# A two-layer decoder trunk on one core: three orders of work shifted by steps (odd heads' scores, a head's first V tile, the roots of the latents' norms)

## The chip, the core and the metric

The kernel runs on one core of one Trainium2 chip. The metric is the device time of one execution in microseconds (us); each version is run several times and the median is compared. Beside the times there is one profiled execution, whose trace gives the start and length of every instruction on the engines: TensorE (PE, with its weight loads as PEld), VectorE (DVE), ScalarE (ACT), GpSimd (POOL) and SyncE (SP, which here only issues transfers).

## What is computed

Two layers over 512 tokens of width 2048, in float32. Layer 0 mixes tokens by retention with 8 heads, layer 1 by latent attention with 16 heads; each has a gate branch, and a condition vector shifts, scales and gates each layer. Cut to what bears on the change:

```python
# layer 0, per head (q, k: 512 x 256 after rotary turning; v: 512 x 512)
scores = (q @ k.T) * decay              # causal, decaying with distance
y = scores @ v
y = (y - mean(y)) * rsqrt(var(y) + EPS) # per token and head
out0 = (silu(g) * y * gn_g) @ w_out
# layer 1
cq, ckv, k_rope, g = split(h @ w_in)    # the latents: 512 x 512 each
q  = rmsnorm(cq, q_norm_g)  @ w_uq
kv = rmsnorm(ckv, kv_norm_g) @ w_ukv
```

## The kernel before

**Arithmetic.** Every float32 operand of a large product is split into a rounded high part and the rest, its low part (`split`, lines 134 to 136: a conversion on ScalarE, L135, then a subtraction on VectorE, L136). A product is three matmuls (`mm3`, lines 156 to 160): high by high (L158), high by low (L159), low by high (L160). The first factor is the loaded weight, the second the moving operand; in a head's values the scores are the weights and V moves, so L158 needs only the high part of a V tile and L159 its low part.

**Steps.** After the first projections the program is a list of `steps` (the class `Step`, line 749). A step has units of weights (a load and a `prepare`, which splits them), a `multiply` of mostly 24 matmuls of 512 columns, a `follow`, and lists of side work, `beside`, under the keys "load", "form" and "multiply". The loop at line 2180 writes each step in this order, and each part stands behind what its engines have already been given (`behind`):

1. SyncE: the weights up to three units ahead, then `beside["load"]`.
2. VectorE and ScalarE: `prepare_for(i + 1)`, the split of the next step's weights.
3. VectorE and ScalarE: `beside["form"]`.
4. TensorE: the step's own matmuls, then `beside["multiply"]`.
5. VectorE: sums of the modulation rows fetched a step before; then the `follow`.

Inside one such part the framework orders instructions by what it thinks is ready; across parts the order stands. Each engine works its queue in order, so VectorE and ScalarE may run ahead of TensorE until something that they need is missing.

**Retention beside the steps.** Heads 0 to 7 do their work beside other products, two heads to a block of 16 steps: the even head's 14 pieces (`retention`, line 1178; list at 1297) lie on steps 0 to 13 of the block, the odd head's on 4 to 17, so its last two reach into the next block (line 1620). Block 0 is the projection of the last q and k (lines 1324 to 1335); the next three are the output projection in rounds of four steps (`round_steps`, line 1412). At a round's end ScalarE copies each PSUM bank away and the next round's sums in (L1358, L1355). Where the pieces meet:

| step of the block | even head | odd head |
|---|---|---|
| 6 | load decay; scores | |
| 8 | load V; decay of the scores (L1223) | |
| 9 | load gates; split V; values | rotary turn |
| 10 | group norm: statistics, root on GpSimd, `yn` (L1262) | load decay; scores |
| 11 | gate (L1268) | |
| 12 | transposes `yT` (L1275) | load V; decay of the scores |
| 13 | output `o_h`, `o_l` (L1292, L1293) | load gates; split V; values |

Scores `s`, values `y` and transposes `yT` each take four PSUM banks out of one set of four (`aux`). Scores are 24 matmuls of 512 to 128 columns, values 30 of 512 columns.

**The latents.** Layer 1's latents, `q` and `kv`, are ready when the steps `g23` begin: eight steps for the third gate group (its products are `x_g`, `s_g`, `z_g`, `y_g`, its weights `g_00e` and so on) and eight for the fourth, 256 columns to a matmul. `latent_norm` (line 1770) stands in the form part of step 0 for `q` and of step 1 for `kv`: four squares with sums on ScalarE (L1775), and `rsqrt` (line 126), which is a small VectorE instruction (L129) and a power on GpSimd (L131). `latent_scale` (L1782, L1784) uses the result in steps 4 and 5.

Of the kernel before, what the change touches and what calls it, by code (L numbers as in the profile page):

```python
# [18 lines left out]
NT = T // P  # L19
# [30 lines left out]
def hybrid_trunk_kernel(  # L50
# [53 lines left out]
    def tmp(name, shape=(P, T)):  # L104
        return base.tile(list(shape), F32, tag="tmp", bufs=6, name=name)
# [7 lines left out]
    def small(name, n=1):  # L113
        return base.tile([P, n], F32, tag="small", bufs=24, name=name)
# [11 lines left out]
    def rsqrt(src, n, mul, name):  # L126

        v = small(f"{name}_v", n)
        DVE.tensor_scalar(out=v, in0=src, scalar1=mul, scalar2=EPS, op0=ALU.mult, op1=ALU.add)  # L129
        r = small(f"{name}_r", n)  # L130
        POOL.tensor_tensor(out=r, in0=v, in1=mhalf[:, :n], op=ALU.pow)  # L131
        return r

    def split(src, hi, lo):
        ACT.copy(hi, src)  # L135
        DVE.tensor_sub(lo, src, hi.bitcast(F32))  # L136
# [304 lines left out]
    A_, V_, T_, S_ = (getattr(mybir.EngineType, e) for e in ("Activation", "DVE", "PE", "SP"))  # L441

    @contextmanager
    def behind(*engines):

        with ExitStack() as stack:
            for e in engines:
                ins = next((i for i in reversed(nc.cur_bb.bb.instructions) if i.engine == e), None)
                if ins is not None:
                    stack.enter_context(tc.issue_after(ins))  # L450
            yield
# [76 lines left out]
    ss = [small(f"x_ss_{t}", 2) for t in range(NT)]  # L528
# [203 lines left out]
    def keep_rows(ps, dst_d, r0, name, func=AF.Identity, own=None):  # L732

        st = lpp.tile([P, T], F32, tag="st", bufs=2, name=name) if own is None else own(name)
        ACT.activation(st, ps, func)
        POOL.dma_start(dst_d[r0 : r0 + P, :], st)
# [12 lines left out]
    class Step:  # L749
# [3 lines left out]
        def __init__(self, load=None, prepare=None, multiply=None, follow=None, rows=0, sums=None):  # L753
            self.units = [(load, prepare)] if load else []
            self.multiply, self.follow = multiply, follow or (lambda: None)
            self.rows, self.sums = rows, sums
            self.beside = {"load": [], "form": [], "multiply": []}

    def plain_steps(nu, kn, parts, cn, name, take, n, lhs, rhs, evac, seeded=False, halved=0, **kw):

# [399 lines left out]
    def l1_tile(tag, bufs, name, shape=(P, T), dt=F32):  # L1160
        return pools["l1"].tile(list(shape), dt, tag=tag, bufs=bufs, name=name)
# [16 lines left out]
    def retention(h, own, own2=None):  # L1178
# [25 lines left out]
        def rope(n, j):  # L1204
            dst = (own2 or own)(f"qk_{h}_{n}_{j}p")
            rope_half(raws[f"qk{n}0"], raws[f"qk{n}1"], j == 1, dst, f"rope_{h}_{n}_{j}")
            qk.append(dst)
# [22 lines left out]
                    s_hl.append((spare[:, 0, 384:512], spare[:, 1, 384:512]))  # L1230
                split(st[:, :n], *s_hl[m])

        def split_v():
            for t in range(NT):
                v.append(own(f"v_{h}_{t}"))
                split(raws[f"v{t}"], v[t][:, 0, :], v[t][:, 1, :])

# [40 lines left out]
        def form_input():  # L1278
# [22 lines left out]
            {},  # L1301
            {"form": lambda: rope(1, 0)},
            {"form": lambda: rope(1, 1)},
            {"load": load_decay, "multiply": scores},
            {},
            {"load": load_v, "form": decay_scores},
            {"load": load_gates, "form": split_v, "multiply": values},
            {"form": group_norm},
            {"form": gate},
            {"multiply": transposes},  # L1310
# [14 lines left out]
    for h in (6, 7):  # L1325
# [3 lines left out]
            lambda b, ps, h=h: keep_rows(  # L1329
                ps, qk_d, (4 * h + b) * P, f"qk{h}_st{b}",  # L1330
                own=tmp,
            ),
# [154 lines left out]
    for u in range(4):  # L1487
        step = Step()
# [105 lines left out]
    for i, (multiply, follow) in enumerate(  # L1594
# [5 lines left out]
        step = Step(multiply=multiply, follow=follow)  # L1600
# [155 lines left out]
    latent = {}  # L1756
# [13 lines left out]
    def latent_norm(n):  # L1770
        if n == "q":
            DVE.tensor_scalar(out=qn_s, in0=qn_c, scalar1=192.0**-0.5, scalar2=None, op0=ALU.mult)
        ss = small(f"ss_{n}", NT)
        for t in range(NT):
            ACT.activation(tmp(f"{n}_sq{t}"), latent[n][t], AF.Square, accum_out=ss[:, t : t + 1])  # L1775
        latent[n, "r"] = rsqrt(ss, NT, 1.0 / 512, f"{n}_r")

    def latent_scale(n):
        for t in range(NT):
            r, v = latent[n, "r"][:, t : t + 1], latent[n][t]  # L1780
            if t % 2:
                ACT.activation(v, v, AF.Identity, scale=r)  # L1782
            else:
                DVE.tensor_scalar(out=v, in0=v, scalar1=r, scalar2=None, op0=ALU.mult)  # L1784
# [27 lines left out]
    def g2_seven(gi):  # L1812


        def load_half(u, odd_, j):
            c0 = 1088 + gi * T + j * H
            return w_mla_in[:, c0 : c0 + H].rearrange("(u i e p) n -> u e p i n", i=2, e=2, p=P)[u, odd_]

        def finish(x, s, y, m4, m5):
            def store(j, half, t):  # L1820
                r0 = (gi * 4 + 2 * j) * P
                POOL.dma_start(
                    sg2_d[r0 : r0 + 2 * P, half * H : (half + 1) * H].rearrange("(b p) n -> p b n", p=P),
                    t.rearrange("p (b n) -> p b n", b=2),
                )

            for j, ps in enumerate((x, s)):
                st = tmp(f"sgs_{gi}_{j}")
                ACT.activation(st, ps, AF.Silu)
                store(j, 0, st)  # L1830
            for j, m in enumerate((m4, m5)):
                DVE.tensor_add(m, m, y)
                ACT.activation(m, m, AF.Silu)
                store(j, 1, m)

        return seven_rows_steps(
            f"g2{gi}", load_half, h2, sums2, *turns2, finish, lambda second, u: 0,
            ((False, 0),) if gi == 2 else ((False, 3), (True, 1)),
        )

    g23 = g2_seven(2) + g2_seven(3)

    for n, g_c, at in (("q", qn_s, (0, 4, 10, 11)), ("kv", kvn_c, (1, 5, 12, 13))):
        g23[at[0]].beside["form"].append(lambda n=n: latent_norm(n))
        g23[at[1]].beside["form"].append(lambda n=n: latent_scale(n))
        g23[at[2]].beside["multiply"].append(lambda n=n: latent_transposes(n))
        g23[at[3]].beside["form"].append(lambda n=n, g_c=g_c: latent_parts(n, g_c))
# [316 lines left out]
    def prepare_for(i):  # L2164
        units = steps[i].units if i < len(steps) else ()
        with behind(V_, A_):
            for _, prepare in units:
                prepare()
        return len(units)
# [10 lines left out]
    for i, step in enumerate(steps):  # L2180
        if i == n_p:
            lp.__exit__(None, None, None)
            l1 = tc.tile_pool(name="l1", bufs=1)
            pools["l1"] = l1.__enter__()
            l1_tile("gap", 1, "gap", (P, EVEN))
        if i == n_l2:
            l1.__exit__(None, None, None)
            l2 = tc.tile_pool(name="l2", bufs=1)
            pools["l2"] = l2.__enter__()
            l2_ready.append(pair_tile(pools["l2"], "own", "own_pair2"))  # L2190
        with behind(S_):
            while n_loaded < min(n_prepared + 3, len(loads)):
                loads[n_loaded]()
                n_loaded += 1
            if i in (n_p, n_l2):
                pool, tables, n0 = (pools["l1"], rotary, 0) if i == n_p else (pools["l2"], rotary2, 2)
                for n, name in enumerate(("cos", "sin")):
                    tables.append(rot(pool, f"{name}_{n0}"))
                    nc.sync.dma_start(tables[n], tables_d[(n0 + n) * P : (n0 + n + 1) * P, :])
            for load in step.beside["load"]:  # L2200
                load()
        n_prepared += prepare_for(i + 1)
        with behind(V_, A_):
            for form_ in step.beside["form"]:
                form_()
        with behind(T_):
            step.multiply()
        with behind(T_):
            for multiply in step.beside["multiply"]:
                multiply()  # L2210
        with behind(V_, A_):
            ahead = 2 if i < n_p - 2 else 1
            for j, add in list(fetched):
                if j + ahead <= i:
                    add()
                    fetched.remove((j, add))
            if step.sums is not None:
                form_sums(step.sums, hT, sums1, staged1, more1)
        if i + 1 < len(steps):
            for _ in range(steps[i + 1].rows):  # L2220
                with behind(S_):
                    fetched += [(i, f) for f in (next(later, None),) if f is not None]
        with behind(V_, A_, T_):
            step.follow()
# [274 lines left out]
```

## Time and profile before

| | |
|---|---|
| median of three runs | 2140.48 us (2140.27 to 2141.76) |
| the profiled execution | 2141.7 us |
| its span, first to last instruction | 2139.9 us |
| mean granted clock of TensorE | 0.998 |

The page of the profile gives busy times and their share of the span. A line of a timeline reads: start in us, length in us, engine, line of the kernel, operation, what is written <- what is read (buffer numbers left out), the shape, how many were merged, and in brackets the engine's idle time ahead and what ended it. A line of the waits reads: who waited <- for whom: us in total, times, longest. Matmuls overlap: one of 512 columns is shown 0.39 us long, but the next one starts well before it ends. So the time that a wait costs is read from start to start.

### The profile page before, as it was taken

To read this page: it belongs to the slowest core of one execution; us is meant where nothing else is said; L and a number is where in the kernel's file an instruction comes from. 1 tells how busy PE (TensorE), PEld (TensorE's weight loads), DVE (VectorE), ACT (ScalarE), POOL (GpSimd) and SP (SyncE) were. 2 spreads that over 40 slices of the span, in tenths; PEclk is the share of its full clock that TensorE was granted. 3 is DMA by queue.
4 is the path that set the end of the run, shared out by engine and by line. 5 is a ranking of instruction groups with operands and counts; after the bars stand their busy time and mean duration, and the time that the engine had idled before them with its cause. 6 is when DMAs were issued, how large, how long until landed. Compare 5 with 4: busy or idle time off the path is not lost. (4 is left out here: it accounts for less than half of the span.)

```text
span 2139.9 us, 29960 instructions
## 1 busy us (share of the span) xinstructions
PE 2114.4 (99%) x11100; PEld 1814.4 (85%) x11100; DVE 1676.8 (78%) x2481; ACT 1054.2 (49%) x1604; POOL 106.4 (5%) x178
## 2 busy tenths in 40 slices
PE   8999999999999999999999999999999999999998
PEld 5887898988888888888888888898889989988887
DVE  7898788888979789666777777668978788886745
ACT  5764444444444544434344544445446565664434
POOL 1000000000000000000000000010001000000000
PEclk9999999999999999999999999999999999999999
DMA  9975687878788778855647566553466644346734
GB/s 382 398 279 193 219 290 229 278 242 262 256 262 265 240 235 277 264 174 192 236 152 249 182 210 240 168 177 113 163 189 205 188 127 148 119 133 221 246 104 143
DMA packets 229781, 462.95 MB, mean 216 GB/s; under 512 B 20817, under 2 KB 84337, under 8 KB 225793
## 3 DMA queue, kind: packets, MB, share of 16 engines
q1 hardware_dynamic: 217424, 421.85, 60.2%
q0 software_dynamic: 11920, 38.91, 4.7%
q8 instruction: 87, 1.43, 0.3%
q14 instruction: 60, 0.49, 0.1%
q10 hardware_dynamic: 290, 0.27, 0.0%
HBM read 417.96 MB, written 43.00 MB: 215 GB/s over the span
## 5 line engine op out<-in xcount | busy, mean ns | idle before, releaser
L1407 PE MATMUL o<-o_h,o_p 128*128 128x512 f32 (+1 forms) x1088 | 323.4, 378 | 0.0
L1407 PEld LDWEIGHTS o<-o_h,o_p 128*128 128x128 f32 x1088 | 199.8, 188 | 37.9 <-DVE o_p L136 1.0
L1407 PE MATMUL o<-o_l,o_p 128*128 128x512 f32 (+1 forms) x544 | 204.8, 376 | 0.0
L1407 PEld LDWEIGHTS o<-o_l,o_p 128*128 128x128 f32 x544 | 102.3, 188 | 18.4
L136 DVE TENSOR_TENSOR o_p<-o_r,o_p 128x1024 fp32r<-128x1024 f32 x64 | 78.1, 1223 | 48.5 <-ACT o_p L135 48.2
L2335 PE MATMUL o<-o_h,o_w 128*128 128x512 f32 (+1 forms) x320 | 82.2, 346 | 0.0
L135 ACT CAST o_p<-o_r 128x1024 fp32r<-128x1024 f32 x64 | 66.5, 1051 | 26.4 <-PE o L1407 15.0
L160 PE MATMUL qk<-hT,qk_p 128*128 128x512 f32 x192 | 75.4, 393 | 1.5 <-DVE qk_p L136 1.5
L158 PE MATMUL qk<-hT,qk_p 128*128 128x512 f32 x192 | 75.8, 395 | 0.0
L159 PE MATMUL qk<-hT,qk_p 128*128 128x512 f32 x192 | 75.3, 392 | 0.0
L378 DVE SCALAR_TENSOR_TENSOR aw<-aw,c_all 128x2048 f32<-128x2048 f32 (+1 forms) x35 | 73.1, 2102 | 2.8 <-DMA aw<-in_ada_t_dram 2.6
L1109 DVE SCALAR_TENSOR_TENSOR mod<-mod,c_odd 128x1024 f32<-128x1024 f32 x48 | 58.0, 1220 | 20.1 <-DMA mod<-in_ada_t_dram 20.1
L2335 PEld LDWEIGHTS o<-o_h,o_w 128*128 128x128 f32 x320 | 55.9, 189 | 7.5
L1109 DVE SCALAR_TENSOR_TENSOR mod<-mod,c_bm 128x1024 f32<-128x1024 f32 x48 | 58.5, 1218 | 0.0
L135 ACT CAST o_h<-o_in 128x1024 fp32r<-128x1024 f32 x24 | 25.2, 1050 | 64.5 <-PE o L159 46.7
L136 DVE TENSOR_TENSOR o_l<-o_in,o_h 128x1024 fp32r<-128x1024 f32 x24 | 29.3, 1222 | 34.1 <-ACT o_h L135 34.1
L2335 PE MATMUL o<-o_l,o_w 128*128 128x512 f32 (+1 forms) x160 | 55.3, 346 | 0.0
L136 DVE TENSOR_TENSOR o_w<-o_w_raw,o_w 128x1024 fp32r<-128x1024 f32 x32 | 38.9, 1220 | 19.0 <-ACT o_w L135 19.0
L1262 ACT ACTIVATE yn<-y,nmr,gn_r 128x512 f32<-128x512 f32 x32 | 22.3, 777 | 62.7 <-DVE nmr L1256 62.7
L159 PE MATMUL o<-o_l,o_w 128*128 128x512 f32 x128 | 50.0, 391 | 0.3 <-DVE o_l L136 0.3
L158 PE MATMUL o<-o_h,o_w 128*128 128x512 f32 x128 | 50.1, 392 | 0.0
L160 PE MATMUL o<-o_h,o_w 128*128 128x512 f32 x128 | 49.9, 390 | 0.0
(1534 smaller groups left out, 6333.6 us busy)
## 6 DMA issues: line engine op xcount, KB each, us to landing
mod<-in_ada_t_dram SPq DMA_DIRECT2D x96, 512.0 KB, 6.0
o_r<-in_ret_w_out_dram SPq DMA_DIRECT2D x64, 512.0 KB, 5.5
aw<-in_ada_t_dram SPq DMA_DIRECT2D x30, 1024.0 KB, 8.9
mod_gate<-in_ada_t_dram SPq DMA_DIRECT2D x32, 512.0 KB, 5.0
o_w_raw<-in_mla_w_out_dram SPq DMA_DIRECT2D x32, 512.0 KB, 4.3
qk_r<-in_ret_w_in_dram SPq DMA_DIRECT2D x48, 256.0 KB, 3.1
qk_r<-qk_d SPq DMA_DIRECT2D x32, 256.0 KB, 6.2
v_r<-v_d SPq DMA_DIRECT2D x32, 256.0 KB, 6.3
```

The lines of the kernel that those rows point to most:

```text
L135: ACT.copy(hi, src)
L136: DVE.tensor_sub(lo, src, hi.bitcast(F32))
L158: PE.matmul(o, lhs[0], rhs[0], start=first and not seeded, stop=False, skip_group_check=seeded)
L159: PE.matmul(o, lhs[0], rhs[1], start=False, stop=False, skip_group_check=seeded)
L160: return PE.matmul(o, lhs[1], rhs[0], start=False, stop=last, skip_group_check=seeded)
L378: DVE.scalar_tensor_tensor(out=aw[:, cols], in0=aw[:, cols], scalar=1.0, in1=c_all[:, cols], op0=ALU.mult, op1=ALU.mult, accum_out=col[:, ...
L1109: DVE.scalar_tensor_tensor(out=aw, in0=aw, scalar=1.0, in1=silu_c[j], op0=ALU.mult, op1=ALU.mult, accum_out=mc[:, j, b : b + 1],)
L1262: ACT.activation(y, ys[i], AF.Identity, bias=nmr[:, i : i + 1], scale=r[:, i : i + 1])
L1407: PE.matmul(o, w[i][:, ki, c0 + b * P : c0 + (b + 1) * P], a[j], start=first and i + j == 0, stop=last and i == 1, skip_group_check=True,)
L2335: PE.matmul(banks2[b][:, cols], w[0][i][:, 0, b * P : (b + 1) * P], o2_moving(w, u, cols)[j], start=u + i + j == 0, stop=u == KD - 1 and i ...
```

## The change

Three shifts; no arithmetic is added or taken away.

1. Of the retention's pieces, `scores` of the odd heads moves from the odd head's piece 6 to piece 7, that is from the end of step 10 of a block to the end of step 11. `load_decay` stays. The even heads stay as they were.
2. `split_v` takes the tiles to be split. A new list `beside["early"]` is written ahead of `prepare_for(i + 1)`. The first V tile of each head is split there, the other three where all four were.
3. `latent_norm` ends at the squares. Its `rsqrt` becomes `latent_root`, in the form part two steps later (step 2 for `q`, step 3 for `kv`).

```diff
-            self.beside = {"load": [], "form": [], "multiply": []}
+            self.beside = {"load": [], "early": [], "form": [], "multiply": []}
...
-        def split_v():
-            for t in range(NT):
+        def split_v(ts):
+            for t in ts:
...
-            {"load": load_decay, "multiply": scores},
-            {},
+            {"load": load_decay} if h % 2 else {"load": load_decay, "multiply": scores},
+            {"multiply": scores} if h % 2 else {},
             {"load": load_v, "form": decay_scores},
-            {"load": load_gates, "form": split_v, "multiply": values},
+            {"load": load_gates, "early": lambda: split_v((0,)), "form": lambda: split_v((1, 2, 3)), "multiply": values},
...
-        latent[n, "r"] = rsqrt(ss, NT, 1.0 / 512, f"{n}_r")
+        latent[n, "ss"] = ss
+
+    def latent_root(n):
+        latent[n, "r"] = rsqrt(latent[n, "ss"], NT, 1.0 / 512, f"{n}_r")
...
         g23[at[0]].beside["form"].append(lambda n=n: latent_norm(n))
+        g23[at[0] + 2].beside["form"].append(lambda n=n: latent_root(n))
...
+        with behind(V_, A_):
+            for form_ in step.beside["early"]:
+                form_()
         n_prepared += prepare_for(i + 1)
```

## The prediction

> **What bounds the kernel now.** I read the page first, then the waits of TensorE and of its weight loads, then the timelines of TensorE, ScalarE and VectorE where a wait was named.
>
> ```profile
> span 2139.9 us, 29960 instructions
> PE 2114.4 (99%) x11100; PEld 1814.4 (85%) x11100; DVE 1676.8 (78%) x2481; ACT 1054.2 (49%) x1604; POOL 106.4 (5%) x178
> PE s L158 <- ACT yn L1262: 1.5, 4, 0.5
> PEld y L159 <- DVE v L136: 1.3, 3, 0.6
> PEld x_g L924 <- DVE g_03e L960: 0.3, 1, 0.3
> ```
>
> TensorE is the bound; only time in which it waits can be won. The edits concern three waits: the scores of the four odd heads (s), which wait for the normalisation of the even head before them; the values (y), which wait for a V tile's low part; and one product of the third gate group (x_g), which waits for weights. Idle time understates such a wait, because matmuls overlap. I measure from start to start:
>
> ```profile
> 966.45 0.39 PE L159 MATMUL qk<-hT,qk_p 128*128 128x512 f32 x1
> 966.67 0.39 PE L160 MATMUL qk<-hT,qk_p 128*128 128x512 f32 x1
> 967.53 0.50 PE L158 MATMUL s<-qk_0p,qk_0p 128*128 128x512 f32 x1 [0.47 <-ACT yn L1262]
> 967.87 0.39 PE L159 MATMUL s<-qk_0p,qk_0p 128*128 128x512 f32 x1
> ...
> 1192.48 0.39 PE L1407 MATMUL o<-o_h,o_p 128*128 128x512 f32 x1
> 1193.22 0.50 PE L158 MATMUL s<-qk_0p,qk_0p 128*128 128x512 f32 x1 [0.36 <-ACT yn L1262]
> 1193.56 0.40 PE L159 MATMUL s<-qk_0p,qk_0p 128*128 128x512 f32 x1
> ```
>
> Undisturbed matmuls of 512 columns start 0.23 us apart (966.45 to 966.67; more finely 0.227, which I use). Head 1's scores start 0.86 us after their predecessor, 0.63 too late, and the next start is 0.34 on, 0.11 too late: 0.74. Head 5: 0.51 + 0.11 = 0.62. The idle of all four is 1.5, less head 1's 0.47 leaves 0.34 each for the rest, so heads 3 and 7 are as head 5. **Scores: 0.74 + 3 x 0.62 = 2.60 us.**
>
> ```profile
> 1179.59 0.39 PE L1407 MATMUL o<-o_h,o_p 128*128 128x512 f32 x1
> 1179.90 1.19 PE L158 MATMUL y<-v,sT 128*128 128x512 f32 x4
> 1181.24 0.50 PE L159 MATMUL y<-v,sT 128*128 128x512 f32 x1 [0.15 <-DVE v L136]
> ...
> 1293.31 0.39 PE L1407 MATMUL o<-o_h,o_p 128*128 128x512 f32 x1
> 1294.96 0.50 PE L159 MATMUL y<-v,sT 128*128 128x512 f32 x1
> ```
>
> Heads 4 and 6 wait for their first V tile. From 1179.59 to 1181.24 lie five steps, 1.14 us; it took 1.65, so 0.51 is lost, and 0.11 behind it as above. Head 6 (1293.31 to 1294.96) is the same. **Values: 2 x 0.62 = 1.24 us.**
>
> ```profile
> 1628.16 0.84 PE L924 MATMUL y_g<-sums,g_02o 128*128 128x256 f32 x6
> 1628.84 1.35 PE L924 MATMUL x_g<-h,g_03e 128*128 128x256 f32 x7
> ```
>
> Six matmuls take 0.84 us, so five steps and a 0.28 matmul, 0.11 a step; seven would be 0.95 and took 1.35. **Third gate group: 0.40 us.** All three together: 4.24 us, which is the most that the edits can win directly.
>
> **Scores of odd heads.** Nothing is added: 24 matmuls go behind the next step's 24. No DMA moves. They waited for PSUM banks that the even head's normalisation still read:
>
> ```profile
> 1192.39 2.78 ACT L1262 ACTIVATE yn<-y,nmr,gn_r 128x512 f32<-128x512 f32 x4 [5.87 <-DVE nmr L1256]
> 1198.73 0.59 ACT L1358 COPY x<-o 128x512 f32<-128x512 f32 x1 [2.62 <-PE o L1407]
> 1203.96 1.04 ACT L135 CAST o_p<-o_r 128x1024 fp32r<-128x1024 f32 x1
> 1206.17 0.68 DVE L1223 TENSOR_TENSOR s_0f<-s,dec 128x512 f32<-128x512 f32 x1
> 1208.97 0.28 DVE L1223 TENSOR_TENSOR s_3f<-s,dec 128x128 f32<-128x128 f32 x1
> 1208.06 1.91 PE L1275 MATMUL yT<-ident,yn 128*128 128x128 f32 x16
> ```
>
> The normalisation ends at 1195.2. The next step would start at 1192.48 + 0.23 = 1192.7 and last 24 x 0.227 = 5.45, so the scores would start at 1198.2: banks free 3 us earlier. The full 2.60 goes. Next late could be the even head's transposes (yT) one step on, which take over the banks of the scores. Scores run 3.7 us (1193.22 to the next step near 1197.1, less the 0.1 restart), so to 1201.9; a step and three of four transposed banks later (5.45 + 1.3) the fourth bank is due at 1208.6. VectorE's decay took from 1206.17 to 1209.25, 3.1 us. It stood behind the 1203.96 conversion, and that behind the round's bank copies, which wait for TensorE (1198.73) and so move up by 3.7 + 0.7 = 4.4 us; behind the normalisation and one conversion they then begin near 1196.1 and, eight of 0.6, end at 1201. Conversion and subtraction (1.05 + 1.2) give 1203.2, the decay ends at 1206.3: 2.3 us of cover. Queued behind the decay on VectorE are a modulation sum, the V split, the next weights and the even head's output; the next consumer is the values at 1201.9 + 5.45 + 1.7 + 5.45 = 1214.5, and that row of work has shorter cover only if the decay stays on its old clock (a rival).
>
> **First V tile ahead of the next weights.** One conversion and one subtraction per head change places with the weights' pair; no instruction and no transfer is added.
>
> ```profile
> 1178.28 1.05 ACT L135 CAST o_p<-o_r 128x1024 fp32r<-128x1024 f32 x1
> 1179.23 2.17 ACT L135 CAST v<-v_r 128x512 fp32r<-128x512 f32 x4
> ...
> 1180.50 2.49 DVE L136 TENSOR_TENSOR v<-v_r,v 128x512 fp32r<-128x512 f32 x4
> ...
> 989.82 0.39 PE L159 MATMUL y<-v,sT 128*128 128x512 f32 x1
> ```
>
> In head 4 tile 0 would be converted at 1178.3 to 1178.9 and subtracted by 1179.7; the values want its low part at 1179.8 + 0.23. That wait goes. But tile 1 is no earlier: its conversion, the weights' pair and tile 0 all still stand ahead of it. Its low part ended at 1180.50 + 2 x 0.60 + 0.09 = 1181.79. Today four products of tile 0 are put first, which hides it; with tile 0 early the order may become the plain one (six products with tile 0, then tile 1), and the eighth is due at 1179.8 + 7 x 0.227 = 1181.4. So 0.37 + 0.11 of wait comes back per head, or 0 if the order stays. I take the returning wait, because head 1, where V is early, already runs in the plain order (its second product, at 989.82, is one with a low part, L159): 1.24 - 2 x 0.48 = **0.3 us**, ends 0.3 and 1.24. The weights behind it come 0.6 to 0.7 us later; they are wanted after 30 value products, 6.8 us.
>
> [...]
>
> **Roots two steps later.** VectorE stood at them:
>
> ```profile
> 1620.06 0.17 DVE L129 TENSOR_SCALAR q_r_v<-ss_q 128x4 f32<-128x4 f32 x1 [1.16 <-ACT q_sq L1775]
> 1625.92 0.17 DVE L129 TENSOR_SCALAR kv_r_v<-ss_kv 128x4 f32<-128x4 f32 x1 [1.24 <-ACT kv_sq L1775]
> 1628.06 1.22 DVE L960 TENSOR_TENSOR g_03e<-g_03e_r,g_03e 128x1024 fp32r<-128x1024 f32 x1
> 1620.31 1.41 POOL L131 TENSOR_TENSOR q_r_r<-q_r_v,few 128x4 f32<-128x4 f32 x1 [82.48 <-DVE q_r_v L129]
> 1636.19 1.33 ACT L1782 ACTIVATE q<-q,q_r_r 128x512 f32<-128x512 f32 x2
> ```
>
> The subtraction ending at 1629.28 is what x_g waits for. Without both idles it can be up to 2.4 us earlier, and 0.4 is enough. The root itself (0.17 on VectorE, 1.41 on GpSimd, no other work of GpSimd between) would end near 1630 against its use at 1636.19. **0.40 us.**
>
> **Sum:** 2.60 + 0.3 + 0.40 = 3.3 us. On the profiled execution (2141.7 us, of which 1.8 lie around its span) that gives 2138.4; it stands 1.2 above the median of the three runs, so the forecast is 2140.48 - 3.3 = **2137.2 us**. About 0.2%, 4.3 us here, is what a measurement of this kernel tells from no change; the forecast is below that.
>
> **Rivals.** (1) *Everything goes*: tile 1 is not late, 4.24 us, 2136.2, a hair from the bound. For: heads 0 and 2 run the same order without a wait. Against: tile 1 has no earlier place. (2) *The transposes take over the wait*: if the decay keeps its old clock, its end at 1209.25 just met the fourth bank (1208.06 + 1.3 = 1209.3); TensorE then arrives 0.6 earlier and waits that long in heads 3, 5 and 7: 3.3 - 1.8 = 1.5 won, 2139.0. Against: the bank copies follow TensorE. (3) *Slower: the early V tile holds the weights.* Place: the conversion queue ahead of the step behind the values, all eight heads.
>
> ```profile
> 1166.52 2.49 SPq L1185 DMA_DIRECT2D v_r<-v_d  x4
> 1201.81 2.22 SPq L1185 DMA_DIRECT2D v_r<-v_d  x4
> DMA to landing us min/median/max: 4.1/6.3/7.4
> ...
> 163.50 0.50 PE L160 MATMUL qk<-hT,qk_p 128*128 128x512 f32 x1 [1.54 <-DVE qk_p L136]
> ...
> 165.46 0.63 PE L160 MATMUL qk<-hT,qk_p 128*128 128x512 f32 x1
> 165.88 0.63 PE L158 MATMUL qk<-hT,qk_p 128*128 128x512 f32 x1
> ```
>
> It decides once V lands later than the next step less 2.3 us of splitting: for head 4 at 1187.1 - 2.3 = 1184.8 (26 products behind 1181.24; V issued at 1166.52, so 18 us), for head 5 at 1214.5 + 6.8 - 2.3 = 1219 (17 us), against 7.4 at most. If it did so by 1.5 us each, a wait as at 163.50 (1.54) would cost 1.7, and behind that one eight matmuls ran 0.42 apart instead of 0.23, 1.6 more: 8 x 3.3 - 3.0 = 23 lost, 2164. [...] The row shows the slow spacing after 1.5 us; I go by the row. (4) *The edits don't reach their waits* (something else ends last at the same places): 2140.5.
>
> **Chances.** Forecast 0.52, (1) 0.22, (2) 0.14, (3) 0.05, (4) 0.07. Rival 1 lies on the bound and half of it counts as faster, with 0.04 for small waits that vanish beside: faster 0.15; slower 0.05 and 0.01 for accidents of a new instruction order: 0.06; within 0.2%: 0.79. The range: below, rival 1 less the half microsecond by which runs differ, 2135.6; above, rival 2 and as much again, 2139.8.
>
> **What would show it.** Right: no wait of s on yn; step 11 of each block follows step 10 at 0.23; scores directly behind; yT without idle; y of heads 4 and 6 with at most 0.4 of a wait, on tile 1's low part; VectorE without the idles of 1.16 and 1.24 ahead of the roots; x_g at 0.11 spacing. Wrong: a wait of yT on the decay, of y on sT, of o on its weights after the values, or scale waiting on the root.

## The result, and the profile after

The changed kernel takes 2135.76 us in the median of 13 runs, beside 2141.14 us for 13 runs of the kernel before: a ratio of 0.9975, 95% interval 0.9968 to 0.9982. That is 5.4 us faster. The forecast was 3.3 us and its range ends at 2135.6, so the time stands at the range's fast edge. The likeliest of the three outcomes, a time within 0.2%, was missed by a hair (0.25% faster, and the interval spans the bound).

The profiled execution took 2134.56 us. The head of its page, and, in the second fence, a line of its waits:

```profile
span 2132.8 us, 29957 instructions
...
PE 2109.9 (99%) x11100; PEld 1814.8 (85%) x11100; DVE 1677.6 (79%) x2481; ACT 1052.8 (49%) x1604; POOL 106.0 (5%) x178
```

```profile
PEld o L159 <- DVE o_l L136: 1.8, 2, 1.0
```

Of the three waits shown of before, s on yn and x_g on g_03e are gone from this list. A wait of 0.3 us of y on v is left of 1.3, in the weight loads alone: no matmul of y idles. The line above has grown from 0.7 us in before to 1.8: the last output waits for the low parts of its inputs (o_l), in a part that no edit touches. TensorE's busy time fell by 4.5 us (from 2114.4) for the same 11100 matmuls: most of the gain never stood as idle.

**The scores of head 5** (timeline of TensorE, after):

```profile
1194.17 0.39 PE L1407 MATMUL o<-o_l,o_p 128*128 128x512 f32 x1
1194.40 0.39 PE L1407 MATMUL o<-o_h,o_p 128*128 128x512 f32 x1
1194.62 0.39 PE L158 MATMUL s<-qk_0p,qk_0p 128*128 128x512 f32 x1
1194.85 0.39 PE L159 MATMUL s<-qk_0p,qk_0p 128*128 128x512 f32 x1
...
1203.65 0.39 PE L1407 MATMUL o<-o_h,o_p 128*128 128x512 f32 x1
1203.88 1.91 PE L1275 MATMUL yT<-ident,yn 128*128 128x128 f32 x16
```

Step 11 stands between, and the scores follow it at 0.22 and 0.23 us; before, the first came 0.74 behind its predecessor (1192.48 to 1193.22). The transposes also follow at 0.23. What they take over is the bank of the last decay (timeline of VectorE, after):

```profile
1202.94 0.28 DVE L1223 TENSOR_TENSOR s_3f<-s,dec 128x128 f32<-128x128 f32 x1
```

It ends at 1203.2, and the fourth bank is due at 1203.88 + 1.3 = 1205.2: 2.0 us of cover.

**The values of head 4, and the last rows of head 7** (timelines of VectorE and of TensorE, after):

```profile
1176.10 0.68 DVE L136 TENSOR_TENSOR v<-v_r,v 128x512 fp32r<-128x512 f32 x1
1176.97 1.23 DVE L136 TENSOR_TENSOR o_p<-o_r,o_p 128x1024 fp32r<-128x1024 f32 x1 [0.18 <-ACT o_p L135]
1178.11 1.89 DVE L136 TENSOR_TENSOR v<-v_r,v 128x512 fp32r<-128x512 f32 x3
...
1323.37 1.88 DVE L136 TENSOR_TENSOR v<-v_r,v 128x512 fp32r<-128x512 f32 x3
```

```profile
1176.91 0.39 PE L158 MATMUL y<-v,sT 128*128 128x512 f32 x1
...
1178.04 0.39 PE L160 MATMUL y<-v,sT 128*128 128x512 f32 x1
1178.27 0.62 PE L158 MATMUL y<-v,sT 128*128 128x512 f32 x2
1178.72 0.62 PE L159 MATMUL y<-v,sT 128*128 128x512 f32 x2
1179.19 0.63 PE L160 MATMUL y<-v,sT 128*128 128x512 f32 x2
...
1322.98 0.39 PE L158 MATMUL y<-v,sT 128*128 128x512 f32 x1
```

Tile 1's low part is ready at 1178.11 + 0.69 = 1178.80. After six products in plain order come pairs: two of L158, two of L159. The first L159 starts at 1178.72, too early for tile 1, so it is tile 0's; tile 1's is the tenth product, at 1178.95, and just in time. Head 7 runs in plain order: there tile 1 is ready at 1323.37 + 0.69 = 1324.06, and its low part is due as the eighth product, at 1322.98 + 7 x 0.227 = 1324.57, 0.5 us later.

**The third gate group** (timeline of VectorE, after, then of TensorE after, then of TensorE before):

```profile
1619.44 1.23 DVE L960 TENSOR_TENSOR g_03e<-g_03e_r,g_03e 128x1024 fp32r<-128x1024 f32 x1
...
1621.71 0.16 DVE L129 TENSOR_SCALAR q_r_v<-ss_q 128x4 f32<-128x4 f32 x1
```

```profile
1622.75 1.52 PE L924 MATMUL x_g<-h,g_03e 128*128 128x256 f32 x12
1624.11 1.52 PE L924 MATMUL y_g<-sums,g_03o 128*128 128x256 f32 x12
...
1640.43 1.52 PE L924 MATMUL x_g<-h,g_13o 128*128 128x256 f32 x12
1641.79 1.52 PE L924 MATMUL s_g<-sums,g_13o 128*128 128x256 f32 x12
```

```profile
1632.03 1.58 PE L924 MATMUL s_g<-sums,g_03e 128*128 128x256 f32 x12
1633.44 1.57 PE L924 MATMUL z_g<-h,g_03o 128*128 128x256 f32 x12
...
1640.51 1.58 PE L924 MATMUL y_g<-sums,g_11e 128*128 128x256 f32 x12
1641.92 1.57 PE L924 MATMUL s_g<-sums,g_11o 128*128 128x256 f32 x12
```

VectorE does not stand at the root, and g_03e ends 2.1 us ahead of its use. But look at the distance between one line of twelve and the next. After: 1.36 us, or 113 ns a matmul. Before, behind the wait of x_g: 1.41 us, or 118 ns, and that still ten microseconds on. Start by start, 332 matmuls ran at 118 there, from 1629.6 to 1668.5, until the latents' transposes come; after, none did. 332 x 4.7 ns = 1.5 us, beside the 0.38 of the wait itself.

**Where the 7.1 us between the two profiles came from.** For this and the experiments I add up, over a stretch (in us from the span's start), by how much each matmul starts later than the columns of the one before it ask for (0.227 us for 512, 0.113 for 256). The texts ahead of the experiments call this the excess. The last two columns are stretches that the change does not touch.

| kernel | time to before, 95% interval | 900–1400 (retention) | 1590–1700 (gate groups) | 150–185 | 2000–2060 |
|---|---|---|---|---|---|
| before | | 5.23 | 2.25 | 3.73 | 0.60 |
| after | 0.9975 (0.9968–0.9982) | 0.59 | 0.40 | 2.10 | 1.56 |
| after, second profile | 0.9975 (0.9965–0.9985) | 1.52 | 0.39 | 2.11 | 0.63 |
| scores alone | 0.9991 (0.9982–1.0) | 2.62 | 2.29 | 2.10 | 0.91 |
| early V alone | 0.9998 (0.9989–1.0007) | 4.79 | 2.25 | 2.09 | 0.61 |
| roots alone | 0.9991 (0.9982–1.0) | 5.01 | 0.39 | 2.11 | 1.27 |
| after + 5 additions | 0.9979 (0.997–0.9988) | 1.04 | 2.79 | 2.09 | 1.58 |
| after + 4 additions | 0.9984 (0.9975–0.9992) | 2.05 | 2.30 | 2.10 | 2.48 |
| + 5 and transposes | 0.9983 (0.9974–0.9992) | 2.55 | 1.67 | 3.71 | 1.49 |
| root of q back | 0.9968 (0.9956–0.9981) | 0.70 | 0.39 | 3.70 | 3.79 |
| gate sums behind | 0.9966 (0.9954–0.9978) | 2.16 | 0.40 | 2.11 | 0.01 |
| early V in even heads | 0.9969 (0.9957–0.998) | 0.69 | 0.42 | 2.12 | 1.59 |
| the last two | 0.9963 (0.9949–0.9976) | 0.59 | 0.40 | 3.70 | 1.80 |
| odd V a step earlier | 1.007 (1.0057–1.0082) | 21.10 | 0.37 | 2.10 | 1.11 |

Retention gave 4.6, the gate groups 1.9, the stretch at 150 to 185 gave 1.6 by luck (below), and the last output took 1.0 back: 7.1.

### The profile page after: what moved, and what is told of

Its sections match the earlier page's. It is cut to its first block, busy times and chain, and to the rows that moved or that the text cites. A ratio compares the mean times of both kernels' runs of the same rounds, so it can differ in the third digit from the quotient of the medians.

```text
span 2132.8 us, 29957 instructions
## 1 busy us (share of the span) xinstructions
PE 2109.9 (99%) x11100; PEld 1814.8 (85%) x11100; DVE 1677.6 (79%) x2481; ACT 1052.8 (49%) x1604; POOL 106.0 (5%) x178
## 4 chain that ended last, share of the span: by engine, by line
PE 90%; DVE 4%; DMA 3%; issue 2%; ACT 1%; POOL 0%; SPq 0%; DVEq 0%; POOLq 0%; ACTq 0%
PE o L1407 16%; PE o L2342 4%; PE s L825 2%; PE y L826 2%; PE y L825 2%; PE y L827 2%; PE s L826 2%; PE s L827 2%; PE x L826 2%; PE x L825 2%; PE x L827 2%; PE qk L160 2%; PE qk L158 2%; PE qk L159 2%; PE v L429 2%
## 5 line engine op out<-in xcount | busy, mean ns | idle before, releaser
L158 PE MATMUL qk<-hT,qk_p 128*128 128x512 f32 x192 | 75.1, 391 | 0.0
L159 PE MATMUL qk<-hT,qk_p 128*128 128x512 f32 x192 | 74.8, 389 | 0.0
L159 PE MATMUL o<-o_l,o_w 128*128 128x512 f32 x128 | 50.1, 391 | 1.0 <-DVE o_l L136 1.0
L158 PE MATMUL o<-o_h,o_w 128*128 128x512 f32 x128 | 50.1, 391 | 0.0
```

The lines of the kernel that those rows point to most:

```text
L158: PE.matmul(o, lhs[0], rhs[0], start=first and not seeded, stop=False, skip_group_check=seeded)
L159: PE.matmul(o, lhs[0], rhs[1], start=False, stop=False, skip_group_check=seeded)
```

## Experiments

**Each shift alone.** The three parts of the diff, one at a time:

```diff
+            {"load": load_decay} if h % 2 else {"load": load_decay, "multiply": scores},
+            {"multiply": scores} if h % 2 else {},
```

> The kernel before with the odd heads' scores one step later and nothing else. Bank theory (the scores waited only for PSUM banks that the even head's normalisation held): the four waits of 0.74, 0.62, 0.62 and 0.62 us vanish, 2.6 us, to a ratio of 0.9988; the waits of the values of heads 4 and 6 (0.62 each) and of x_g (0.4) stay, and the 256-column matmuls behind x_g keep the spacing of 118 ns that they have before. Rival (the wait moves on to the transposes one step later): 0.6 us in each of three heads comes back, 0.8 us won, 0.9996.

Measured: 2.61 us less in the retention, and the waits of y and x_g as before. The four waits of the scores are theirs, and 2.60 was their size.

```diff
+            {"load": load_gates, "early": lambda: split_v((0,)), "form": lambda: split_v((1, 2, 3)), "multiply": values},
```

> The kernel before with each head's first V tile split ahead of the next step's weights and nothing else. If all of the values' wait was the first tile's low part: 1.24 us won, 0.9994, no start of a y product more than 0.05 us late. If the second tile is late next, as the prediction had it: 0.3 us won and 0.4 us of wait left in each of heads 4 and 6. The scores' waits stay at 2.6 us, x_g at 0.4.

Measured: both y waits went, 1.24 us, but only 0.44 was won. The rest came back one step on; a line of the waits and one of TensorE's timeline, early V alone:

```profile
PE s L158 <- ACT yn L1262: 2.5, 4, 0.9
```

```profile
1191.26 0.50 PE L158 MATMUL s<-qk_0p,qk_0p 128*128 128x512 f32 x1 [0.89 <-ACT yn L1262]
```

The scores of heads 5 and 7 now wait 1.05 (start to start) instead of 0.52. The last product of head 4's values starts 2.50 us earlier than before on the span's clock (1184.54, from 1187.04), the normalisation only 1.96 (1190.43, from 1192.39): its statistics stand on VectorE behind the split of other weights, with no idle ahead of them, so they did not get earlier with the values, and what the values gave the scores took. Early V pays because the scores' shift has put a step between; alone, its time (0.9998) can't be told from before. I had not foreseen this: the waits were added up as if each were its own.

```diff
+        g23[at[0] + 2].beside["form"].append(lambda n=n: latent_root(n))
```

> The kernel before with the roots of the latents' norms two steps later and nothing else. Rhythm theory (a wait inside a stretch of 256-column matmuls leaves them 118 ns apart instead of 113 until matmuls of another kind come): the x_g wait of 0.4 us goes, and with it 332 x 4.7 ns = 1.5 us, together 1.9 us in the trace between the start of the third gate group and the first transposes of the latents, ratio 0.9991; the spacing there is 113 ns throughout. Rival (the spacing of 118 has another cause, traffic or an accident of that one execution): 0.4 us, 0.9998, spacing not tied to the wait.

Measured: 1.87 us less in the gate groups, not 0.4. Timeline of TensorE, roots alone:

```profile
1627.01 1.52 PE L924 MATMUL x_g<-h,g_03e 128*128 128x256 f32 x12
1628.37 1.52 PE L924 MATMUL y_g<-sums,g_03o 128*128 128x256 f32 x12
```

Twelve every 1.36 us, and all 455 matmuls of that stream at 113 ns.

**Is it the wait that sets the spacing?** The result of the additions in these kernels, and of the transposes, is not used.

```diff
+    def delay(n):
+        d = tmp("delay")
+        for _ in range(n):
+            DVE.tensor_add(d, latent["q"][0], latent["q"][0])
+    g23[1].beside["form"].append(lambda: delay(5))
```

> The changed kernel with five additions on scratch (about 3.0 us of VectorE, their result is not used) behind the forming work of step 1 of the third gate group, so that the low part of the weights g_03e is late again by another cause, by about 0.7 us. Rhythm theory: the wait costs 0.7 and the stretch behind it runs at 118 ns up to the transposes, 1.5 us more; 2.2 us slower than the changed kernel, ratio to the kernel before about 0.9985. Rival (the spacing has nothing to do with the wait): 0.7 us slower than the changed kernel, spacing 113 ns, about 0.9978.

Measured: a wait of 0.82 + 0.11, and behind it 330 matmuls at 118 ns (1624 to 1663); 2.39 us more than after. The time (0.9979) can't tell the theories apart, the spacing does.

```diff
-    g23[1].beside["form"].append(lambda: delay(5))
+    g23[1].beside["form"].append(lambda: delay(4))
```

> The kernel after, with four VectorE additions (their result is not used) in the form part of the second step of the third gate group, one fewer than in the kernel with five. Each is worth about 0.6 us of delay, so the subtraction of g_03e, with five of them 0.9 us late, would be 0.2 to 0.4 late. Theory 'rhythm' (a wait in these 256-column products puts all that follow on 118 ns instead of 113, however short it is): the short wait itself plus the whole 1.5 us, so the excess of 1590 to 1700 rises from 0.40 to 2.0 to 2.4 and the stretch at 118 ns still holds some 330 matmuls. Rival 'a wait costs its own length only, or in proportion': excess 0.7 to 1.2, and a stretch at 118 that is much shorter or absent. In time against the kernel before: 0.9983 by the first, 0.9977 by the second, which the times alone will hardly tell apart; the spacing will.

Measured: a wait of 0.32 + 0.11, and 332 matmuls at 118. Timeline of TensorE, four additions:

```profile
1624.29 1.45 PE L924 MATMUL x_g<-h,g_03e 128*128 128x256 f32 x10 [0.15 <-DVE g_03e L960]
...
1626.99 1.57 PE L924 MATMUL s_g<-sums,g_03e 128*128 128x256 f32 x12
1628.40 1.58 PE L924 MATMUL z_g<-h,g_03o 128*128 128x256 f32 x12
```

A wait shown as 0.15 us of idle cost 1.9 us: 0.4 of it at once, 1.5 in small change. The slow stretch was as long behind the wait of 0.32 us (332 matmuls) as behind that of 0.82 (330).

```diff
+    def reset():
+        ps = aux("reset")
+        for i in range(4):
+            PE.transpose(ps[:, i * P : (i + 1) * P], ident, ident)
+    g23[4].beside["multiply"].append(reset)
```

> The kernel with five additions (wait of 0.82 us, then some 330 matmuls at 118 ns, excess 2.79 over 1590 to 1700), and four transposes of the identity into a bank that nobody reads, behind the products of the fifth step of the group (near 1640 us). Theory 'rhythm, ended by other matmuls' (the stretch ends where the latents' transposes come, because they break the stream): the spacing returns to 113 ns behind the four transposes; about 190 matmuls fewer at 118, 0.9 us won, against some 0.45 for the transposes themselves. Rival 'it ends by its own clock or at the products' end': 118 ns stays on both sides of the transposes up to 1663, excess about 3.2. In time both are within 0.02% of the kernel with five additions.

Measured: 78 matmuls at 118 ahead of the four transposes, 250 at 113 behind them. Timeline of TensorE, five additions and transposes:

```profile
1635.12 1.58 PE L924 MATMUL s_g<-sums,g_10o 128*128 128x256 f32 x12
1636.54 0.60 PE L1861 MATMUL reset<-ident 128*128 128x128 f32 x4
...
1638.34 1.52 PE L924 MATMUL y_g<-sums,g_11e 128*128 128x256 f32 x12
1639.70 1.52 PE L924 MATMUL s_g<-sums,g_11o 128*128 128x256 f32 x12
```

From 1635.12 to 1636.54 twelve take 1.42; from 1638.34 to 1639.70 1.36. So in this run other matmuls ended the slow stretch; without them, with five additions alone, it still held after 330, where the latents' transposes come. What TensorE does in it stays open. A wait is also not the only thing that slows this stream: in both kernels some lines of twelve run at 120 ns with no wait ahead (in after the first two of the group, at 1606.28 and 1607.71, and the first and third behind each set of the latents' transposes). They are the same before and after, so they don't bear on the difference.

**Are both roots needed late?**

```diff
-        g23[at[0] + 2].beside["form"].append(lambda n=n: latent_root(n))
+        g23[at[0] + (2 if n == "kv" else 0)].beside["form"].append(lambda n=n: latent_root(n))
```

> The kernel after, with the root of q alone in its old place; that of kv stays two steps later. VectorE then stands idle at the root of q for about 1.2 us once. The subtraction of g_03e ended at 1620.7 in the kernel after and is wanted at 1622.75, 2.1 us of cover, so it ends near 1621.9, still in time. Theory 'one root later is enough': no wait of x_g, 113 ns throughout, excess of 1590 to 1700 stays at 0.4, time as the kernel after (0.9975). Rival 'both idles count' (the queue behind it is delayed by more than the idle): a wait comes back, and with it the 118 ns, excess 1.9 to 2.3, 0.9984.

Measured: no wait, 113 ns throughout. Timeline of VectorE, then of TensorE:

```profile
1615.19 0.17 DVE L129 TENSOR_SCALAR q_r_v<-ss_q 128x4 f32<-128x4 f32 x1 [1.16 <-ACT q_sq L1775]
...
1622.00 1.22 DVE L960 TENSOR_TENSOR g_03e<-g_03e_r,g_03e 128x1024 fp32r<-128x1024 f32 x1
```

```profile
1623.97 1.52 PE L924 MATMUL x_g<-h,g_03e 128*128 128x256 f32 x12
```

VectorE stands 1.16 us again, g_03e ends at 1623.22 and is wanted at 1623.97. One idle may stay, and 0.75 us of cover is left.

**The gate sums of the last output.**

```diff
     def o2_hooks(i):
         l2_hooks.get(i, lambda: None)()
+
+    def o2_gates(i):
         with behind(V_):
             while gate_pending:
...
         if k not in o2_split:
             o2_split[k] = o2_parts(*k)
+        o2_gates(r * (KD // 2) + u if r < 2 else KD)
         return wt, o2_split[k]
```

> The kernel after, with the loads and sums of the last layer's modulation gates moved behind the split of the same step's weights and inputs of the last output projection. In the kernel after, VectorE stands at such sums while their transfer is late, and the low parts of the inputs (o_l) queue behind: 0.57 + 0.11 near 2018 and 0.74 + 0.11 near 2024. Theory: these two waits go, the excess of 2000 to 2060 falls from 1.56 (0.6 to 1.6 in the other kernels) to about 0.3, and the kernel is 0.3 to 1.2 us faster than after: 0.9970 to 0.9974. Rival: the sums are due soon behind, or the weights queue on the transfers, and a wait comes back at another place: excess 0.6 or more, 0.9975 or above.

Measured: 0.01 in the last stretch, which looked like the theory. The same edit in the kernel of both edits (below) had 1.80. Timeline of VectorE there:

```profile
2013.29 1.23 DVE L2070 SCALAR_TENSOR_TENSOR mod_gate<-mod_gate,c_gate 128x1024 f32<-128x1024 f32 x1 [2.27 <-DMA mod_gate<-in_ada_t_dram]
...
2014.44 1.22 DVE L136 TENSOR_TENSOR o_l<-o_in,o_h 128x1024 fp32r<-128x1024 f32 x1
```

A sum whose row is late still stands ahead of o_l. It does in the first profile of the edit too (a sum waits 1.30 us for its row, then o_l follows at 2012.50), only that there nothing came too late. So the edit did not put the late sums behind, and the 0.01 is not shown to be its work. This theory falls.

But the same profile held something else: the values of head 7 wait. Timelines of ScalarE after, of ScalarE with the gate sums behind, and of TensorE there:

```profile
1317.98 0.62 ACT L135 CAST v<-v_r 128x512 fp32r<-128x512 f32 x1 [2.54 <-DMA v_r<-v_d]
1318.51 1.05 ACT L135 CAST o_p<-o_r 128x1024 fp32r<-128x1024 f32 x1
1319.46 2.41 ACT L1292 ACTIVATE o_h<-yT,vcol 128x512 fp32r<-128x512 f32 x4
1321.75 1.67 ACT L135 CAST v<-v_r 128x512 fp32r<-128x512 f32 x3
```

```profile
1319.04 0.62 ACT L135 CAST v<-v_r 128x512 fp32r<-128x512 f32 x1 [3.44 <-DMA v_r<-v_d]
```

```profile
1325.16 0.50 PE L159 MATMUL y<-v,sT 128*128 128x512 f32 x1 [0.29 <-DVE v L136]
```

This is the forecast's slower rival at work: the early tile holds ScalarE until its transfer lands, in heads 3, 5 and 7 (0.97, 2.13 and 2.54 us in after). The next weights, the even head's output and the head's own other tiles queue behind it. In after that was just covered. Where V was converted 1.06 us later, tile 1 came 0.45 + 0.11 too late. Of seven profiles with all early tiles and the scores' shift two show it. It takes both edits: with early V alone ScalarE waits for V nowhere. From early V alone to after, the conversion ahead of head 7's tile ends 5.75 us earlier (1315.45, from 1321.20), while V's transfer is issued only 1.77 us earlier (1311.66, from 1313.43).

```diff
+            {"load": load_gates, "form": lambda: split_v((0, 1, 2, 3)), "multiply": values} if h % 2
+            else {"load": load_gates, "early": lambda: split_v((0,)), "form": lambda: split_v((1, 2, 3)), "multiply": values},
```

> The kernel after, with the first V tile of the even heads alone split early; odd heads split all four tiles where the kernel before does. In the kernel after, ScalarE stands at the early tile of the odd heads 3, 5 and 7 until its transfer lands (0.97, 2.13 and 2.54 us), and in two of the six profiles with that edit and the scores' shift the values of head 7 then wait 0.45 to 0.54 + 0.11 for their second tile. Theory 'the early tile of odd heads holds the queue' : ScalarE's three waits for V's transfer go, no y wait in any head (heads 4 and 6 keep their early tile, odd heads had no such wait before), excess of 900 to 1400 between 0.6 and 1.1, time 0.9972 to 0.9976. Rival 'all heads need it': a wait of some 0.5 comes at the odd heads' values, excess above 1.5, 0.9977 or more.

Measured: ScalarE waits for V nowhere, no y wait in any head, 0.69 in the retention; the time, 0.9969, is not to be told from that of after. Odd heads never needed the early tile.

The two edits above (gate sums behind, early V in even heads) together:

> The last experiment's even-head V edit and the modulation gates of layer 1 behind the split of the output's weights, on the kernel after. If both are what they seem, the excess of 900 to 1400 is 0.6 to 1.1, that of 2000 to 2060 at most 0.1, and the time is 0.9962 to 0.9970. If the gain of the gates' edit was chance, it is 0.9975.

Measured: 0.9963, the lowest ratio of all, but its interval overlaps that of after, and its profile lost 1.80 us at the gates. That it beats the changed kernel is not shown; that it beats the one before is.

```diff
+            {"load": load_v, "early": lambda: split_v((0,)) if h % 2 else None, "form": decay_scores},
+            {"load": load_gates, "early": lambda: None if h % 2 else split_v((0,)), "form": lambda: split_v((1, 2, 3)), "multiply": values},
```

> The kernel after, with the odd heads' early V tile one step earlier still, ahead of the weights of the values' own step. V is issued where it was (its transfer stands behind a modulation row on SyncE), so in heads 3, 5 and 7 ScalarE stands until it lands, and the weights behind it are converted and subtracted 2.8 us later: near 1320.8 in head 7's clock, against 1317.7, when TensorE comes to them. Theory 'a late V tile holds everything behind it': three waits of o of about 3 us, excess of 900 to 1400 up by 9 to 10 from 0.6, and 1.6 more for each wait behind which the clock falls: 1.0018 to 1.0045. Rival, as the slower case of the forecast had it ('V lands long before what is behind it is due, 14 us of cover less one step of 5.5'): no wait, 0.9975. Between them: the modulation sums and transfers shift too, and one or two heads wait, 0.999 to 1.001.

Measured: 1.007, some 20 us slower than after. The waits, and head 7 in the timeline of TensorE:

```profile
ACT v L135 <- DMA v_r<-v_d: 25.9, 3, 9.1
...
PE yT L1275 <- DVE s_0f L1223: 14.5, 3, 6.0
```

```profile
1328.49 0.39 PE L1407 MATMUL o<-o_h,o_p 128*128 128x512 f32 x1
1334.85 3.53 PE L1275 MATMUL yT<-ident,yn 128*128 128x128 f32 x16 [5.97 <-DVE s_0f L1223]
1338.13 0.47 PE L1407 MATMUL o<-o_h,o_p 128*128 128x512 f32 x1
```

Three waits, as expected, but of the transposes and not of the output's weights: the decay stands behind the held weights on VectorE, and it is due sooner. Start to start they lose 3.49, 5.31 and 6.14 us, 14.9 in all. Behind the last the sixteen transposes run 0.21 apart instead of 0.11 (3.53 us, not 1.91): the granted clock is 0.50 from 1334 to 1338, which costs some 1.6 us more. It is 0.64 from 1214 to 1218.5 too. Three times 1.6 beside the 14.9 makes 19.7, by estimate, of the 20.5 us by which the retention lost more than in after.

> The kernel after, unchanged, for a second profile. What belongs to the change must come again: excess of 1590 to 1700 at 0.4 with 455 matmuls at 113 ns, no wait of s on yn, no y wait in heads 4 and 6, ScalarE standing 5 to 7 us in all at V's transfer. If the rest is chance of one execution, it differs from the first profile in at least one of four places: the clock behind the wait at 163 (full in the first), small waits for output weights near 1247 to 1266 (none in the first, up to 1.2 elsewhere), the values of head 7 (no wait in the first, 0.56 to 0.65 in two kernels of the same retention), the low parts of the last inputs near 2018 (1.56 in the first, 0 to 3.8 elsewhere). Rival: these belong to each kernel's order of instructions, and all four come as in the first. Time 0.9970 to 0.9980.

Measured: what belongs to the change came again (gate groups 0.39, no wait of s; ScalarE stood 5.8 us at V). Two of the four other places differ: small waits for output weights near 1247 to 1264 (0.6 us), and 0.63 at the last inputs instead of 1.56.

## Why the forecast held, and where it did not

- **Scores, 2.60: right**, by 2.61 alone, and by the way it was said to come: banks free well ahead, step 11 at normal spacing.
- **Transposes: right.** 2.3 us of cover was worked out, 2.0 stands in the trace. The bank copies moved up: the first starts at 1193.01 right behind a conversion, where in before ScalarE idled 2.62 us ahead of it. Rival 2 did not happen.
- **Values, 0.3: wrong; 1.24 went.** The failed step is the choice that tile 1's wait comes back in heads 4 and 6, taken because head 1 already runs in the plain order. Tile 1 would indeed have been too late for the plain order (ready at 1178.80, the eighth product at 1178.50). But the order there is not the plain one: pairs begin after the sixth, and tile 1's low part is needed by the tenth, at 1178.95. That the order came out so, with 0.15 us to spare, was not foreseen: it is luck. The returning wait is real where the order is plain: it is head 7's, when V is late.
- **Third gate group, 0.40: mis-sized; 1.9.** That the wait goes, and that one idle less is enough, was right. The term counted the wait and not the pace of the 332 matmuls behind it, though the trace of before showed both: from 1632.03 to 1633.44 twelve take 1.41, and ahead of the wait six take 0.68 (1628.16 to 1628.84), which is 1.36 for twelve.
- **The slower rival: the mechanism is there, its point of decision was wrong.** It was put at the weights of the step behind the values, 17 or 18 us from V's issue. What decides first is nearer: the even head's output and tiles 1 to 3 queue behind the early tile too, and V lands, in heads 3, 5 and 7, after ScalarE has come to it (by 0.97, 2.13 and 2.54 us). Of cover, 0.5 us was left in head 7. It costs 0.6 us in some executions, and 20 us when the tile is put one step further up.
- **The price of a wait's slow clock: not regular.** Windows of TensorE from 160 to 180, before and then after:

```profile
160.00:180.00 20.00, 18.46 (x73) 0.91 0.57 191
```

```profile
160.00:180.00 20.00, 18.45 (x80) 1.00 0.58 196
```

The columns are the stretch, its length, PE's busy time and matmuls, the granted clock, and the DMA's share and GB/s. The wait at 163 took 1.71 us in before and 1.72 in after (start to start), and in all fourteen profiles TensorE is busy 18.45 to 18.47 us of this stretch; behind it the granted clock fell in four of them (0.91 here in the mean, before among these), and not in ten (1.00). So 1.6 of the 7.1 us between the profiles is no gain. "I go by the row" took one execution's row for a rule. In before the clock is 0.50 from 164.44 to 167.85, a spell that begins 0.9 us behind the end of the wait, and eight matmuls start 0.42 apart in it; ahead of it and behind it the clock is full. Why the same wait was followed by this in four executions and not in ten was not shown.
- **The sum.** Terms of 2.60, 1.24 and 1.9 make 5.7. The retention gave 0.8 more than its two: half of that is four small waits for output weights near 1257 to 1268 (0.41 in before, none in after, 0.6 in its second profile), which come and go between executions; the other half is spread over late starts of under 0.08 each. Measured alone, the three save 2.61, 0.44 and 1.87 in their stretches; together early V is worth its full 1.24, as the scores no longer take it back.
- **The range: held by luck.** From the forecast's base of 2140.48 us the same 5.4 us would end at 2135.1, below the range; the time lies inside because 13 runs put before at 2141.14. The lower end allowed for the "half microsecond by which runs differ", but the 13 runs of before lie between 2138.78 and 2144.39, and it had no term for the slow pace behind x_g.

## What to carry to other kernels

Price a wait from the first late start to the place where the old spacing is back: in the gate groups of before the pace behind a wait of 0.38 us cost 1.5 us more. Waits in a chain are not added up one by one; ask of each what the time won runs into next. And before work is put ahead in an engine's queue, see when its transfer lands against when the engine comes to it, and look for the nearest consumer of everything queued behind, not for the one that it was moved past.

## What the runs showed of the hardware

- The 256-column stream of the gate groups ran at 113 ns from start to start, and at 118 ns once one of its matmuls had waited, be it by 0.27 us (before) or by 0.32 or 0.82 us (four and five additions). Behind four 128-column transposes (five additions and transposes) 250 matmuls ran at 113 again. Lines of twelve at 120 ns stand in both kernels without a wait (1606.28 and 1607.71 in after). The 512-column stream showed no such change (0.227 us ahead of the wait of head 5's scores and behind it). The cause is open.
- The length of a wait alone did not tell whether the granted clock fell. The 1.71 us at 163 was followed by a fall in four profiles of fourteen; in before it was 0.50 from 164.44 to 167.85, 3.41 us. Near 36, TensorE waited 2.31 us in after (up to 36.37), and the clock was 0.50 from 36.76 to 40.17, again 3.41 us; it waited 2.41 us in before (up to 36.17), and the clock stayed at 1.00 (33 to 40). With odd V a step earlier it was 0.50 in the mean from 1334 to 1338, of which 0.85 us lay still within the wait of 6.14 us, and 0.64 from 1214 to 1218.5.
